# Four one-word loads behind the second pair's stores, and which completion semaphores the later stores get

## The chip, the cores and the metric

One core of one Trainium2 chip. The metric is the device time of one execution in microseconds; the kernel before takes 126.50 us (median of three runs, 126.49 to 126.56). Runs are marked fast or slow (a run over 1.5% above the fastest of the same kernel is slow), and only fast ones are compared. A profiled execution also gives a *span*, some 1.8 us shorter than the time, in which all positions below are counted.

## The reference

```python
def reference(x, weight):            # x: 16 x 64 x 64 x 64, weight: 128 x 64 x 3 x 3, 90% zeros
    x_pad = np.pad(x, ((0, 0), (0, 0), (1, 1), (1, 1)))
    for b, co, ci, kh, kw in ...:
        if weight[co, ci, kh, kw] != 0:
            output[b, co] += weight[co, ci, kh, kw] * x_pad[b, ci, kh:kh+h, kw:kw+w]
```

It is a 3x3 convolution with padding 1. The kernel treats it as dense.

## The kernel before

Two images make a pair; eight pairs follow each other. Input comes by GpSimd's queue, which casts to bf16 on the way (15.73 MB in FP32 by the shapes, 7.86 MB in its packets); output leaves by SyncE's queue, 2 MB for each image.

```python
    const_pool = ctx.enter_context(tc.tile_pool(name="const", bufs=1))
    x_pool = ctx.enter_context(tc.tile_pool(name="x", bufs=1))
    ...
    o_pool = ctx.enter_context(tc.tile_pool(name="o", bufs=7))
    ...
    nc.sync.dma_start(out=w_sb, in_=weight.rearrange("o i kh kw -> o (i kh kw)"))
    x_head = o_pool.tile([128, H, W], FP32, name="o")
    nc.sync.dma_start(out=x_head[:, 0:HEAD, :], in_=pair(0)[:, 0:HEAD, :])
    ...
    for p in range(NP):
        o = [o_pool.tile([C_OUT, H, W], FP32, name="o") for _ in range(2)]
        last = p == NP - 1
        for blk in range(4):
            ...                                   # products on TensorE, sums on VectorE into o
            if last and blk % 2 == 1:
                for n in range(2):
                    rows = slice(r0 - 16, r0 + 16)
                    nc.sync.dma_start(out=out[2 * p + n][:, rows, :], in_=o[n][:, rows, :])
        if not last:
            for n in range(2):
                nc.sync.dma_start(out=out[2 * p + n], in_=o[n])
```

What the source does not show: in the built program every transfer that SyncE issues takes the next of eight completion semaphores, its *slot*, in turn, and waits first for the transfer that had the slot before (the trace's records of its 20 transfers name the semaphores). After its last store SyncE waits for the slots 0, 1, ..., 7 in this order (116.25 to 123.85 us), and only then, at 123.97 us, does it join the closing barrier of all engines.

## Time and profile before

| | before |
|---|---|
| time, median | 126.50 us |
| span | 124.7 us |
| last addition on VectorE ends | 112.0 us |
| last data packet ends | 123.12 us |
| last completion lands | 123.59 us |
| from there to the end of the span | 1.155 us |

How the DMA time is divided, from the queue part of the page (packets, MB, share of 16 engines' span):

```profile
q1 hardware_dynamic: 2880, 34.90, 66.6%
q0 software_dynamic: 1296, 7.86, 30.8%
...
HBM read 17.07 MB, written 33.55 MB: 406 GB/s over the span
```

q1 is SyncE's queue, q0 GpSimd's. Together they fill 97% of the sixteen engines' span, so no idle stretch is left that earlier issues could fill; what can become shorter are the fixed ends.

### The profile page before, as it was taken

What the parts mean: (1) busy time and instruction counts of PE and PEld (TensorE: products, weight loads), DVE (VectorE), ACT (ScalarE), POOL (GpSimd) and SP (SyncE); (2) the same over time, 40 slices, a digit from 0 to 9 for tenths busy, and PEclk for the clock granted to TensorE, in tenths of its full rate; (3) what the DMA queues carried; (4) which work ended last, traced back from release to release, by engine and by line L of the source; (5) the groups of instructions that cost most, each with busy time, mean ns of one, the idle gap of its engine ahead of it and who ended that gap; (6) DMA issues with size and microseconds to landing.
All of it is one profiled execution on the core that took longest, in us unless ns stands there. A gap on an engine that the chain in (4) does not pass through costs nothing.

```text
span 124.7 us, 2543 instructions
## 1 busy us (share of the span) xinstructions
PE 109.0 (87%) x1030; PEld 59.5 (48%) x1030; DVE 82.3 (66%) x135; ACT 39.0 (31%) x71; POOL 41.1 (33%) x46
## 2 busy tenths in 40 slices
PE   6999999999999999999999999999999999940000
PEld 6755555555555555555555555555555555510000
DVE  0354777877787778777877787778777878870000
ACT  4545323333333333333333333333333333300000
POOL 6427343533353335333533333333333300000000
PEclk9999999999999999999999999999999999998555
DMA  4999999999999999999999999999999999999991
GB/s 127 356 225 213 215 218 213 211 400 311 350 409 410 318 297 344 436 310 323 302 433 310 318 315 423 420 449 420 426 431 420 436 426 441 415 412 420 428 381 53
DMA packets 4188, 42.93 MB, mean 344 GB/s; under 512 B 464, under 2 KB 464, under 8 KB 976
## 3 DMA queue, kind: packets, MB, share of 16 engines
q1 hardware_dynamic: 2880, 34.90, 66.6%
q0 software_dynamic: 1296, 7.86, 30.8%
q8 instruction: 8, 0.13, 0.4%
q14 instruction: 4, 0.03, 0.1%
HBM read 17.07 MB, written 33.55 MB: 406 GB/s over the span
## 4 chain that ended last, share of the span: by engine, by line
PE 82%; DMA 5%; DVE 1%; issue 1%; DVEq 0%; SPq 0%
PE ps L148 82%; DMA o<-in_x_dram 5%; DVE o L181 1%; DVEq L233 0%; DVE x L99 0%; SPq L60 0%; DVEq L181 0%
## 5 line engine op out<-in xcount | busy, mean ns | idle before, releaser
L181 DVE TENSOR_TENSOR o<-ps,pc 128x512 f32<-128x512 f32 x124 | 77.8, 686 | 22.1 <-PE ps L148 19.8
L148 PE MATMUL ps<-x,wT 64*128 64x504 bf16 (+3 forms) x780 | 88.7, 373 | 0.3 <-DVE x L99 0.3
L148 PEld LDWEIGHTS <-wT 64*128 64x128 bf16 x966 | 54.4, 94 | 48.9 <-issue 0.3
L167 POOL TENSOR_TENSOR s<-x 128x512 bf16<-128x512 bf16 x31 | 35.6, 1151 | 57.5 <-PE ps L148 43.2
L174 ACT COPY pc<-ps 128x512 f32<-128x512 f32 x62 | 33.3, 589 | 64.0 <-issue 61.8
L148 PE MATMUL ps<-s,wT 64*128 64x512 bf16 (+1 forms) x186 | 25.7, 377 | 0.0
L84 PE MATMUL ps<-idle_rhs 128*128 128x128 bf16 x55 | 4.8, 265 | 1.0 <-DVE idle_rhs L79 1.0
L84 PEld LDWEIGHTS <-idle_rhs 128*128 128x128 bf16 x55 | 4.4, 123 | 1.0 <-DVE idle_rhs L79 1.0
L68 POOL DMA_DIRECT2D x<-in_x_dram x8 | 4.4, 561 | 0.0
L103 DVE CAST w_bf<-w_sb 128x192 bf16<-128x192 f32 (+1 forms) x4 | 1.1, 346 | 2.9 <-DMA w_sb<-in_weight_dram 2.9
L162 DVE COPY o<-ps 128x512 f32<-128x512 f32 x2 | 1.4, 692 | 2.0 <-PE ps L148 2.0
L161 ACT COPY o<-ps 128x512 f32<-128x512 f32 x2 | 1.2, 586 | 2.4 <-PE ps L148 2.4
L99 ACT CAST x<-o 128x576 bf16<-128x576 f32 (+1 forms) x2 | 1.5, 804 | 0.8 <-DMA o<-in_x_dram 0.8
L99 DVE CAST x<-o 128x576 bf16<-128x576 f32 x1 | 0.5, 460 | 1.9 <-DMA o<-in_x_dram 1.9
L103 ACT ACT_TABLE_LOAD x1 | 1.3, 1283 | 0.7 <-PEq L222 0.7
L109 PE MATMUL ps<-ident,w_bf 128*128 128x128 bf16 x9 | 1.1, 296 | 0.3 <-DVE w_bf L103 0.3
L103 ACT CAST w_bf<-w_sb 128x64 bf16<-128x64 f32 (+1 forms) x2 | 0.7, 416 | 1.8 <-DMA w_sb<-in_weight_dram 1.8
L109 PEld LDWEIGHTS <-w_bf 128*128 128x128 bf16 x9 | 0.8, 128 | 0.7 <-DVE w_bf L103 0.7
L113 DVE TENSOR_TENSOR wT<-ps,wT 128x384 bf16<-128x384 f32 x2 | 1.0, 548 | 0.0
L63 POOL DMA_DIRECT2D x<-in_x_dram x1 | 0.7, 693 | 0.8 <-POOLq L222 0.8
L79 DVE MEMSET idle_rhs<- 128x64 uint32 x1 | 0.1, 112 | 0.8 <-PEq L222 0.8
L122 ACT CAST wT<-ps 128x384 bf16<-128x384 f32 x1 | 0.5, 480 | 0.4 <-PE ps L109 0.4
(8 smaller groups left out, 2.0 us busy)
## 6 DMA issues: line engine op xcount, KB each, us to landing
out_dram<-o SPq DMA_DIRECT2D x14, 2048.0 KB, 17.4
x<-in_x_dram POOLq DMA_DIRECT2D x6, 1024.0 KB, 15.8
out_dram<-o SPq DMA_DIRECT2D x4, 1024.0 KB, 11.4
o<-in_x_dram SPq DMA_DIRECT2D x1, 1024.0 KB, 5.6
x<-in_x_dram POOLq DMA_DIRECT2D x1, 640.0 KB, 14.0
x<-in_x_dram POOLq DMA_DIRECT2D x1, 512.0 KB, 7.5
x<-in_x_dram POOLq DMA_DIRECT2D x1, 384.0 KB, 24.6
w_sb<-in_weight_dram SPq DMA_DIRECT2D x1, 288.0 KB, 3.0
```

Source lines behind the costliest of these rows:

```text
L68: nc.gpsimd.dma_start(out=xs[p][:, a:b, :], in_=pair(p)[:, a:b, :])
L84: nc.tensor.matmul(idle_ps, idle_rhs, idle_rhs, start=True, stop=True)
L99: copy(out=xs[0][:, a:b, :], in_=x_head[:, a:b, :])
L103: copy(out=w_bf4[:, g, a:b, :], in_=w_v[:, k : k + b - a, :])
L109: nc.tensor.matmul(wps[:, j, :], src, ident, start=True, stop=True)
L113: nc.vector.tensor_tensor(out=wT[:, g], in0=wps, in1=wT[:, G1], op=SUB)
L148: nc.tensor.matmul(ps[n][:, lo:hi, c_lo:c_hi], tap(g, kw, n), src[q, a:b:step, c_lo + kw - 1 : c_hi + kw - 1], start=(i == 0), stop=(i == ...
L161: nc.scalar.copy(out=o[0][:, r0 : r0 + rows, :], in_=ps[0])
L162: nc.vector.tensor_copy(out=o[1][:, r0 : r0 + rows, :], in_=ps[1])
L167: nc.gpsimd.tensor_tensor(out=s, in0=xs[p][:, r0 : r0 + 16 : 2, :], in1=xs[p][:, r0 + 1 : r0 + 16 : 2, :], op=ADD)
L174: nc.scalar.copy(out=c, in_=shared[n])
L181: nc.vector.tensor_tensor(out=o[n][:, first : r0 + 16 : 2, :], in0=ps[n], in1=pc[n], op=ADD)
```

## The change

The intent: four transfers with as good as no data push all later transfers on SyncE's queue four slots on.

```diff
         if not last:
             for n in range(2):
                 nc.sync.dma_start(out=out[2 * p + n], in_=o[n])
+        if p == 1:
+            spare = const_pool.tile([1, 4], FP32, name="spare")
+            for k in range(4):
+                nc.sync.dma_start(out=spare[:, k : k + 1], in_=weight[0:1, 0, 0, 0:1])
```

The last four stores have slots 0 to 3 before and 4 to 7 after. As a side effect the tile moves all x and o tiles by 32 bytes.

## The prediction

> **What bounds the kernel now.** I read the head of the page first, then the slices, the DMA queues, the chain that ended last, what SyncE's queue waited for, and last a table by stretches of time.
>
> ```profile
> PE 109.0 (87%) x1030; PEld 59.5 (48%) x1030; DVE 82.3 (66%) x135; ACT 39.0 (31%) x71; POOL 41.1 (33%) x46
> ...
> PE   6999999999999999999999999999999999940000
> ...
> DMA  4999999999999999999999999999999999999991
> ```
>
> Two resources look full. TensorE is at 9 from the second slice on, but its last four slices (12.5 us) are empty; the DMA engines are at 9 from the second slice to the last but one. What stands at the end decides.
>
> ```profile
> PE 82%; DMA 5%; DVE 1%; issue 1%; DVEq 0%; SPq 0%
> ...
> 7.35 102.09 PE ps L148 x954
> ...
> 111.38 0.60 DVE o L181
> ```
>
> The chain is 82% TensorE, which invites "TensorE-bound". But it ends at 111.98 us with the last addition, and the span is 124.7 us. The remaining 12.7 us are no engine's work:
>
> ```profile
> 112.00:122.80 10.80, 0.00 (x0) 0.00 (x0) 0.00 (x0) 0.00 (x0) 0.00 (x0) 0.62 0.90 379
> 122.80:123.59 0.79, 0.00 (x0) 0.00 (x0) 0.00 (x0) 0.00 (x0) 0.00 (x0) 0.50 0.03 10
> 123.59:124.70 1.11, 0.00 (x0) 0.00 (x0) 0.00 (x0) 0.00 (x0) 0.00 (x0) 0.50 0.00 0
> ```
>
> Here the engines' columns are all zero; the last two columns are the DMA share and GB/s. DMA is busy to 122.8 us, then there is a completion delay, then 1.1 us in which nothing moves. The volume agrees: 17.07 MB read plus 33.55 MB written is 50.6 MB, in about 120.8 us (2.0 to 122.8), which is 419 GB/s; stretches late in the run (80 to 112 us) show 426. So I take the kernel as bound by the DMA engines nearly from first to last, with TensorE just ahead of them. The fixed end comes after that.
>
> ```profile
> SPq L207 <- DVE o L181: 90.1, 14, 20.1
> SPq L233 <- DMA out_dram<-o: 10.4, 4, 3.2
> SPq L204 <- DVE o L181: 10.1, 4, 4.9
> ```
>
> SyncE, which issues all stores, waits before each store for VectorE's result and for nothing else (14 + 4 waits). No store was ever held by a completion semaphore. Only the program's closing waits are DMA waits: four of them, 10.4 us. The closing waits of SyncE in 123.60 to 123.88 us:
>
> ```profile
> L233 SPq EVENT_SEMAPHORE  x5: 28/28/28, 123.6 to 123.8; - x5
> ```
>
> The trace has their starts at 123.607, 123.666, 123.728, 123.787 and 123.849 us: the first is the wait that the last store ended, the other four found their semaphores long satisfied and cost 59 to 65 ns each.
>
> [...] The trace agrees on the queueing: stores take a median 17.4 us to land though one moves in about 4.9 us (2 MB at 425 GB/s). [...]
>
> **The change part by part.**
>
> *The slots.* The built program hands HWDGE transfers eight completion semaphores in turn, and each transfer first waits for the one that had its slot eight transfers before. Before, weight and first input took slots 0 and 1, the 18 stores 2 to 7, 0 to 7, and 0 to 3. After, four loads take 6, 7, 0, 1 behind the second pair; the last four stores then have slots 4 to 7.
>
> *Waits before stores.* The third pair's two stores now wait for the first pair's (landed at 34.7 and 41.0 us), at 47.4 us, when VectorE releases them. The fourth pair's (60.2 us) wait for the second pair's (50.2 and 56.8 us). The fifth pair's and sixth pair's wait for the four loads, issued about 36 us, so done by some 57 us, against 73.0 and 85.8 us. The seventh pair's (98.6 us) wait for the third pair's (61.4 to 64.8 and 68.5 to 73.3 us). The last four wait for the same stores as before. Every wait is satisfied by 3 us or more: cost 0. VectorE's own waits for free output buffers name other semaphores but the same stores; the order of instructions is the same on all engines but SyncE.
>
> *The four loads themselves.* SyncE's time: it issues stores in 0.33 to 1.35 us and idles from about 36 us to 47 us, so four issues of such a size, 1.3 to 5.4 us, are hidden. Engine time: the smallest records in before's trace are four-byte ones, 9 to 12 ns on the hardware queue (semaphore writes) and 22 ns on the software queue. Four loads of a data and a semaphore record, by those, are 4 x (22 + 12) = 0.14 us[...]. The last store's 16 completions are spread over 2.61 us, and the slowest stands 0.28 us behind the next. So by chance, with one engine in sixteen being the last, the expected cost is about 0.01 us, and at the worst 0.14 us by this estimate.
>
> *The end.* SyncE closes by waiting for slots 0 to 7 in this order (with others that are done). Before, the last four stores sit in slots 0 to 3, so the four satisfied waits for 4 to 7 come after the last landing, on the path: 4 x 61 ns = 0.24 us. After, the satisfied slots 0 to 3 are passed while stores drain, and the wait for slot 7 is the last. Gain 0.24 us of the 1.1 us.
>
> *The spare tile.* Built, it takes 32 bytes of each partition below the x and o tiles; x0 moves from 24704 to 24736 and the first o tile from 101504 to 101536. [...]
>
> Sum: -0.24 + 0.01 + 0.08 = -0.15 us; 126.50 - 0.15 = 126.35, which I put down as 126.3 since I trust the first term most.
>
> **The rivals.**
>
> *Stores issue earlier, because waits are re-paired.* This is what the title suggests at first reading. If slot waits held stores, a gap of several microseconds in DMA could close. Against it: 18 of 18 store waits are VectorE's, and the DMA row has no gap to be filled. It would make nothing of the time.
>
> *Tiny loads are dear.* [...] Against: packets overlap in the trace (the DMA share reads 1.03 in places)[...]. I give this 2%.
>
> *A new wait.* The loads could land so late that the fifth pair's stores wait. They would need to take 37 us (36 to 73); no transfer in the trace took over 25.3. If so, only SyncE waits, behind a DMA queue that still holds the pair before, and little is lost.
>
> *The 32-byte shift changes the rate.* If all transfers lost 1%, that is 1.2 us, 127.5: still within 2%. Nothing in the profile speaks for it[...].
>
> **Range and chances.** The runs of before lie within 0.07 us (126.49 to 126.56). The gain is bounded by 0.24 us unless something unforeseen happens, the costs mostly by 0.3; other chips and builds may move it by 0.3% (0.4 us). So 125.9 to 126.9 for 8 in 10. Two per cent is 2.5 us: only dear loads get there. Faster 0.01, within 0.97, slower 0.02.
>
> **What would show it.** Four store waits at the end ended by DMA as before, and the last of them followed at once by the drain: one closing semaphore wait of SyncE's, not five, behind the last landing, and 0.9 us from it to the end instead of 1.15. SyncE's waits for stores still all on VectorE. DMA still full to about 122.8 us, PE busy 109.0. Wrong would be: a DMA wait at L207; the last store's landing later than 123.6 us by more than 0.3; or the same 1.1 us of silence at the end.

The sum came to -0.24 + 0.01 + 0.08 = -0.15 us, so 126.35. The +0.01 us is an estimate, a sixteenth of 4 x (22 + 12) ns = 0.14 us; the 0.14 us is the worst case, all four loads on the engine that finishes last, which no record shows. The 0.3% for other chips was an allowance: the medians of the kernel before on three chips were 126.50 to 126.61 us.

## The result, and the profile after

126.35 us, median of six runs, against 126.50 us of the kernel before in the same rounds; one of the six is slow, and the median of the five fast ones is 126.21 us. Ratios here are the mean time of one kernel's fast runs over that of the other's in the same rounds, so not quite the ratio of the medians; this one is 0.9985, with a 95% interval of 0.997 to 1.0. The slow run took 131.57 us; such a run also came to the kernel before, in a later comparison (130.8 us), and the ratios leave them out.

The same three stretches at the end, from a table by stretches (columns: us; busy time of TensorE, its weight loads, VectorE, ScalarE, GpSimd with counts; clock; DMA share; GB/s):

```profile
112.00:122.80 10.80, 0.00 (x0) 0.00 (x0) 0.02 (x1) 0.00 (x0) 0.00 (x0) 0.60 0.90 381
122.80:123.41 0.61, 0.00 (x0) 0.00 (x0) 0.00 (x0) 0.00 (x0) 0.00 (x0) 0.50 0.00 0
123.41:124.32 0.91, 0.00 (x0) 0.00 (x0) 0.00 (x0) 0.00 (x0) 0.00 (x0) 0.50 0.00 0
```

The bulk is the same (0.90 of the DMA engines, 381 for 379 GB/s). The silent last stretch is 0.91 us where it was 1.11 in the same view (1.155 and 0.912 us from the records, from the last landing). The closing waits of SyncE between 123.40 and 123.70 us:

```profile
L240 SPq DRAIN  x2: 7/7/7, 123.5 to 123.6; - x2
...
L240 SPq EVENT_SEMAPHORE  x1: 28/28/28, 123.4 to 123.4; - x1
```

One semaphore wait and then at once the drain; before there were five. SyncE comes to its closing waits ten microseconds earlier, while the stores drain (113.0 to 113.3 us):

```profile
L240 SPq EVENT_SEMAPHORE  x4: 28/28/28, 113.1 to 113.2; - x4
```

The first of these four is a wait for other semaphores, the next three (113.12 to 113.25 us) are those for slots 0 to 2. Slot 3 was not yet free: it ended at 113.65 us, with the seventh pair's second store (landed at 113.63 us), and this cost nothing, as four stores were still to land.

What SyncE's queue waited for in the whole run (us in total, times, longest):

```profile
SPq L207 <- DVE o L181: 85.7, 14, 20.2
SPq L240 <- DMA out_dram<-o: 10.0, 5, 2.4
SPq L204 <- DVE o L181: 9.9, 4, 4.8
SPq L207 <- DMA out_dram<-o: 0.8, 1, 0.8
```

The last line is new: once SyncE did wait for a slot ahead of a store. The records tell which: at 49.4 us it had issued the third pair's stores and went on to the wait for the second pair's first store, which landed at 50.125 us; it passed at 50.142. The store behind it was due at 60.2 us, so this wait lies within one for VectorE and cost nothing.

The loads:

```profile
L214 SPq DMA_DIRECT2D spare<-in_weight_dram x4: 1008/1300/1453, 36.1 to 39.8; - x4
```

They took SyncE 5.2 us to issue (36.07 to 41.27 us), in a gap that lasts to 47.4 us, and landed at 52.97 to 53.52 us, 13.7 to 16.9 us after each was issued. Between each load's issue and this landing its semaphore shows exactly two updates, the first 0.12 to 0.17 us after the issue ends and the second 12.1 to 15.6 us later. (A store's shows sixteen.) Who wrote which the trace does not say.

### The profile page after: what moved, and what is told of

The parts are those of the page before. It is cut to its first block, busy times and chain, and to the rows that moved or that the text cites. A ratio compares the mean times of both kernels' runs of the same rounds, so it can differ in the third digit from the quotient of the medians.

```text
span 124.3 us, 2549 instructions
## 1 busy us (share of the span) xinstructions
PE 108.9 (88%) x1030; PEld 59.8 (48%) x1030; DVE 82.2 (66%) x135; ACT 39.0 (31%) x71; POOL 41.1 (33%) x46
## 3 DMA queue, kind: packets, MB, share of 16 engines
q1 hardware_dynamic: 2888, 34.90, 66.8%
## 4 chain that ended last, share of the span: by engine, by line
PE 82%; DMA 5%; DVE 1%; issue 1%; DVEq 0%; SPq 0%
PE ps L148 82%; DMA o<-in_x_dram 5%; DVE o L181 1%; DVEq L240 0%; DVE x L99 0%; SPq L60 0%; DVEq L181 0%
```

## The experiments

Twelve kernels, each in five rounds beside the kernel before on the same chip (its medians were 126.61, 126.58 and 126.50 us, each on another chip; the first covers four_again to five_loads, the second eight_loads to split_stores, the third the other four). "Behind" is the number of closing semaphore waits of SyncE from the one that the last landing ends; "tail" is the time from the last landing to the end of the span, of the profiled run. The medians include slow runs; without them they are 126.21 us for the changed kernel, 126.58 for twelve_loads, 126.61 for pe_later, 127.08 for split_stores and 132.6 for split_rows.

| run | last stores' slots | loads | median us | ratio to before, 95% | behind | tail us |
|---|---|---|---|---|---|---|
| before | 0-3 | 0 | 126.50 | | 5 | 1.155 |
| changed kernel | 4-7 | 4 | 126.35 | 0.9985 (0.997 to 1.0) | 1 | 0.912 |
| four_again | 4-7 | 4 | 126.38 | 0.9983 (0.9969 to 0.9998) | 1 | 0.899 |
| loads_no_shift | 4-7 | 4 | 126.22 | 0.9972 (0.9959 to 0.9985) | 1 | 0.903 |
| tile_only | 0-3 | 0 | 126.39 | 0.9989 (0.9976 to 1.0002) | 5 | 1.145 |
| five_loads | 5-7, 0 | 5 | 126.77 | 1.0016 (1.0003 to 1.003) | 8 | 1.341 |
| eight_loads | 0-3 | 8 | 126.51 | 0.9995 (0.9983 to 1.0007) | 5 | 1.140 |
| twelve_loads | 4-7 | 12 | 126.94 | 1.0017 (0.9988 to 1.0046) | 1 | 0.904 |
| pe_later | 0-3 | 0 | 126.65 | 0.9998 (0.9983 to 1.0012) | 5 | 1.154 |
| split_stores | 4-7 | 0 | 127.10 | 1.0039 (1.0027 to 1.0051) | 1 | 0.898 |
| split_rows | 4-7 | 0 | 136.0 (132.5 to 141.3) | 1.0476 (1.0444 to 1.0509) | 1 | 0.898 |
| twenty_loads | 4-7 | 20 | 126.75 | 1.002 (0.9986 to 1.0054) | 1 | 0.904 |
| twentyeight_loads | 4-7 | 28 | 126.40 | 0.9988 (0.9968 to 1.0007) | 1 | 0.927 |
| four_own_pool | 4-7 | 4 | 126.25 | 0.9974 (0.9956 to 0.9991) | 1 | 0.899 |

My theory was the closing order: the gain is the satisfied waits that no longer stand behind the last landing. The rivals: the loads or the moved tiles gain in themselves; the spread of runs; and, for the premise, that TensorE and not DMA sets the end.

### The change once more

Edit: none.

> The changed kernel itself, once more on this chip. Theory (closing order: the four satisfied waits of 59 to 65 ns leave the path): 0.24 us under the kernel before, ratio about 0.998; one closing semaphore wait after the last landing. Rival (spread of runs only): no difference, ratio 1.000.

Measured: 126.38 us, ratio 0.9983; one wait behind, tail 0.899 us. The gain came back in the size of the first comparison, and this interval lies wholly below 1, narrowly (0.9998).

### Loads without moving the tiles

```diff
+    spare_pool = ctx.enter_context(tc.tile_pool(name="spare", bufs=1))     # after o_pool
...
-            spare = const_pool.tile([1, 4], FP32, name="spare")
+            spare = spare_pool.tile([1, 4], FP32, name="spare")
```

> The same four loads into a tile that lies behind the o tiles, so no other tile moves by 32 bytes. Theory: all of the gain stays, about -0.24 us. Rival (the 32-byte move did it): no gain, 126.5. [...]

Measured: 126.22 us, ratio 0.9972, and later with other rivals once more:

> Four loads behind the second pair with their tile behind the o tiles, once more, on the same chip as its rivals here: 126.2 by the earlier run, one closing wait behind the last landing. Rival (the earlier 126.22 against 126.38 was chance): 126.4.

126.25 us, ratio 0.9974. The gain doesn't need the move of the tiles. By the ratios it is 0.35 and 0.33 us here. That it is more than the 0.24 us of the tail isn't shown, since a ratio of 0.9981 lies in both intervals; nor is it shown to be more than in the changed kernel, as the intervals overlap (0.9956 to 0.9991 for the two here, 0.9969 to 0.9998 for the repeat).

### The tile without loads

```diff
     make_identity(nc, ident)
+    spare = const_pool.tile([1, 4], FP32, name="spare")
+    nc.gpsimd.memset(spare, 0.0)
```

> The spare tile alone, written once by GpSimd at the start, no load; all later tiles 32 bytes further. Theory: closing waits as before (five in a row behind the last landing)[...]. Rival (the 32-byte move did it): 126.3.

Measured: ratio 0.9989 with an interval that includes 1; its closing waits between 123.51 and 123.80 us:

```profile
L235 SPq EVENT_SEMAPHORE  x5: 28/28/28, 123.5 to 123.8; - x5
```

Five behind the landing, tail 1.145 us, as before. No cost of the move was seen; a gain of up to 0.24% isn't excluded by the interval, but the tail didn't take part in it. The expectation on record was about 126.5 us; the range that is cut from it rested on a cost of the move that no trace shows. Nor do the packets show one: of the 1792 packets of 16384 bytes, 1242 took exactly 611 ns before, 1238 in the changed kernel and 1241 here.

### Five loads: the worst order

```diff
-            for k in range(4):
+            for k in range(5):                     # tile of 5 words, in spare_pool
```

> Five loads in place of four, tile behind the o tiles. The last store then has slot 0, the first in the closing order, and seven satisfied waits (1 to 7) stand behind it. Theory: 3 x 61 ns = 0.18 us over the kernel before, 126.7, and 0.43 us over the four loads. Rival (loads or their place gain time in themselves): same as with four, 126.3.

This is the sharpest test, since one load more should turn the gain into a loss. Measured: 126.77 us, ratio 1.0016, which is 0.20 us more by the ratio and 0.16 by the medians (126.61 for the kernel before); 0.18 was expected. The waits of SyncE, and its closing semaphore waits between 123.96 and 124.43 us:

```profile
SPq L241 <- DMA out_dram<-o: 10.7, 1, 10.7
SPq L208 <- DMA out_dram<-o: 10.2, 3, 6.8
```

```profile
L241 SPq EVENT_SEMAPHORE  x8: 28/28/28, 124.0 to 124.4; - x8
```

SyncE stands 10.7 us at the wait for slot 0, which the very last store ends, and then passes eight waits in a row, the other seven long satisfied. From the landing to the drain that is 0.511 us, against 0.324 with five and 0.081 with one: (0.511 - 0.081) / 7 = 0.061 us for each satisfied wait. The rival that loads gain in themselves falls.

The second line shows another rival for the loss: with five loads each store waits for a more recent transfer, and the third pair's second store, which the kernel before issued at 47.98 us, was held by its slot and issued at 50.90 us, 2.9 us later. It doesn't explain the loss: from 44 to 62 us the DMA share stays at 0.98 to 1.05, and the rates of that stretch add up to 6.01 MB against 6.03 before, an estimate of 0.05 us. twentyeight_loads is a harder test: there the fifth pair's stores were issued at 76.05 and 77.12 us in place of 72.99 and 73.59, behind loads, and the time is 0.15 us over that with four loads, all that 24 more loads cost included. With other stores still in the queue, stores issued some 3 us late cost next to nothing here.

### Eight loads: the slots turned full circle

```diff
-        if p == 1:
+        if p in (1, 4):                            # four loads each, in spare_pool
```

> Four loads behind the second pair and four behind the fifth, tiles behind the o tiles: the slots are back where the kernel before has them for the last four stores (0 to 3). Theory: the gain is gone, 126.5 (+0.0 to +0.1 for the loads), five closing waits behind the last landing. Rival (loads in themselves gain): 126.3 or less.

Measured: 126.51 us, ratio 0.9995; between 123.60 and 123.88 us:

```profile
L241 SPq EVENT_SEMAPHORE  x5: 28/28/28, 123.6 to 123.9; - x5
```

The gain is gone with the old slots, though there are twice the loads.

### What a load costs: twelve, twenty and twenty-eight

```diff
-        if p == 1:
+        if p in (0, 1, 4):                         # twelve_loads
```
```diff
+    early = spare_pool.tile([1, 12], FP32, name="early")      # behind x_head's load
+    for k in range(12):
+        nc.sync.dma_start(out=early[:, k : k + 1], in_=weight[0:1, 0, 0, 0:1])
...
+        if p in (1, 4):                            # twenty_loads; (1, 2, 3, 4) for twentyeight_loads
```

> Four loads behind each of the first, second and fifth pair: the last stores have slots 4 to 7 as with four loads, and three times the loads. Theory (a load costs next to nothing): 126.3, within 0.1 us of four loads. [...] at 0.034 us each, as estimated, by 0.4 us on one engine, at most 126.6.

(The 0.4 us is an estimate, 12 x 0.034 us, if all fall on one engine.)

Twelve loads: the tail is that of slots 4 to 7 (0.904 us), but the fast runs fall in two groups: 126.35, 126.48 and 126.58, and 127.31 and 127.36. The profiled run was one of the low ones. In its trace, as in the others with loads, four loads in a row land 0.18 to 0.19 us apart (92.060, 92.247, 92.430, 92.613), five times what I had put down for one. My guess was that a load holds its engine for so long, and that with twelve the engine sometimes becomes the last. The next two kernels were to show it:

> Twelve loads at the very start and four each behind the second and fifth pair; last stores in slots 4 to 7. Theory A (a load takes one engine 184 ns, the spacing at which consecutive loads land): 20 x 0.184 = 3.7 us on that engine; the 16 completions of the last store are 2.5 us apart, so the end moves by 1.2 us (that engine first) to 3.7 us (last): 127.4 to 129.9. Theory B (the spacing is only latency, the engine works on beside it; 0.034 us each as predicted): 126.3 to 126.9.

> Twelve loads at the start and four behind each of the second to fifth pairs; same slots. Theory A: 8 x 0.184 = 1.47 us over the kernel with twenty, 129 to 131. Theory B: 126.3 to 127.2.

Measured: 126.75 us with twenty (six runs from 126.19 to 127.60), 126.40 us with twenty-eight (126.37 to 126.64). Theory A falls: 28 x 0.184 = 5.2 us on one engine would stand out by at least 2.6 us, as the sixteen completions of the last store are only 2.6 us apart in the kernel before. The time with 28 loads is 0.15 us over that with four (126.40 and 126.25), so even if their engine was the first to finish, they set it back by no more than 2.6 + 0.15 us, which is an estimate of at most 0.1 us a load. Both steps take all loads to use the same engine, which is the assumption: no record names the engine. If it holds, the 0.184 us is the rhythm of landings, not the price; it was not shown.

The loads as such don't explain the upper group of twelve_loads or the scatter of twenty_loads, because more of them scatter less. In the profiled run of twenty_loads (127.37 us) the first input landed 1.5 us later (TensorE's products begin at 8.91 us and not at 7.35), and the packets of SyncE's queue in 22 to 36 us moved 24.0 bytes/ns against 26.3 before. But fifteen of the last store's sixteen completions are in by 123.21 us (123.31 in the kernel before), and one alone comes 1.04 us behind them, at 124.25, and makes this run long. Whose it is, and why, is open; split_stores, without loads, has the same picture.

### TensorE 2 us later

```diff
         last = p == NP - 1
+        if p == 5:
+            late_ps = psum_pool.tile([128, 128], FP32, name="ps")
+            for _ in range(32):
+                nc.tensor.matmul(late_ps, idle_rhs, idle_rhs, start=True, stop=True)
```

> The kernel before with 32 idle 128x128 matmuls in front of the sixth pair, some 2 us of TensorE in the middle of the run; no loads. Theory (bound by the DMA engines, which still have over 9 us of stores queued when VectorE ends): the same, 126.5, and only VectorE's end moves, from 112.0 to 114.0 us. Rival (TensorE's chain sets the end): +2 us, 128.5.

Measured: ratio 0.9998. The last step of the chain that ended last:

```profile
113.41 0.60 DVE o L181
```

It was at 111.38 us before. The engines end 2.03 us later and the time stays: TensorE, 82% of "the chain that ended last", isn't what ends last.

### The same slots without loads

```diff
-            if last and blk % 2 == 1:
+            if (last or p < 2) and blk % 2 == 1:
...
-        if not last:
+        if not last and p >= 2:
```

> No loads: the stores of the first two pairs are issued in halves, four transfers more, all of them useful, and the last four stores get slots 4 to 7 as in the changed kernel. Theory: the same gain of 0.24 us, 126.3 (earlier stores share the DMA engines with loads, which move no fewer bytes for it). Rival (the loads matter, not the slots): 126.5.

Measured: 127.10 us, ratio 1.0039: a miss. The tail did as the theory has it (one wait, 0.898 us), but the last landing is at 124.34 us, 0.75 later than before. The DMA engines were busy for 122.69 us each in the mean, against 121.95: the 0.74 us were made by the transfers. In part by shorter rows: a packet of 8192 bytes takes 309 ns and one of 16384 takes 611, so two halves cost 7 ns more than a whole, and 4 stores x 8 rows an engine (128 over 16, in the mean) x 7 ns is an estimate of 0.22 us. The rest isn't explained; of the last store's sixteen completions fifteen are in by 123.36 us (123.31 before), and one alone stands 0.98 us behind (0.28 before). So I cut along partitions next, with whole rows:

```diff
+            cuts = ((0, 64), (64, 128)) if p < 2 else ((0, 128),)
             for n in range(2):
-                nc.sync.dma_start(out=out[2 * p + n], in_=o[n])
+                for a, b in cuts:
+                    nc.sync.dma_start(out=out[2 * p + n][a:b], in_=o[n][a:b])
```

> No loads: each store of the first two pairs is issued as two, partitions 0 to 63 and 64 to 127, so rows stay 16 KiB long; four transfers more, last four stores in slots 4 to 7. Theory (slots matter, and the stores in halves lost by their 8 KiB rows): 126.25, the gain of 0.24 us without a load's cost. Rival (more transfers cost as such): 127.1 as with the stores in halves.

Measured: 132.54 to 141.26 us in six runs, of which two count as fast; the ratio 1.0476 is of these two. The run scatters so widely (clocks 0.907 to 0.947) that only its direction is to be relied on. Again the tail is the short one (0.898 us) and the loss is in the transfers. While the half stores are under way, before and in this kernel, in the table by stretches:

```profile
22.00:35.00 13.00, 13.00 (x126) 6.86 (x122) 10.23 (x17) 4.49 (x10) 5.31 (x6) 1.00 1.02 321
```

```profile
22.00:35.00 13.00, 13.00 (x125) 6.92 (x122) 10.23 (x17) 4.49 (x9) 5.30 (x6) 1.00 1.02 253
```

The engines' work is the same and the DMA share is the same 1.02, but 253 GB/s move in place of 321: each packet takes longer. On SyncE's queue a packet moved 17.6 bytes/ns from 22 to 36 us, where it was 26.3. The mechanism was not looked for further. Here the halves cost 4.8% of the time by the ratio of the two runs that count as fast. What it shows: nearly empty transfers were the cheap way to move the slots, and useful ones weren't.

## Why the prediction was right

**The bound.** Shown by pe_later: 2 us of TensorE in the middle cost no more than 0.15 us by the interval, so TensorE does not set the end; the stores that still drain then do.

**The closing order, -0.24 us.** Shown. The tail is 0.90 to 0.93 us in all nine profiles with one wait behind the landing, 1.14 to 1.155 in the four with five, and 1.34 with eight. The changed kernel's tail became 1.155 - 0.912 = 0.243 us shorter. Times follow: a gain with four loads (four comparisons of four, of which the first has an interval that reaches 1.0), none with eight, a loss with five. One detail was off: slot 3 was still waited for when SyncE came to it, without cost.

**The waits before stores, 0.** Right in the time, wrong in one statement. The prediction held that all of SyncE's waits at stores would stay VectorE's and called a DMA wait there a sign of error. There is one, of 0.8 us. The step behind it compared each landing with the time at which the store was due, and that is the right comparison for the cost; but SyncE comes to a slot's wait earlier, as soon as the store ahead is issued. So the sign was badly chosen, not the step. In five_loads and twentyeight_loads stores really went out late, by 2.9 and up to 3.5 us, and the DMA engines did not run dry: the cost of 0 stands on firmer ground than the reason given for it, that all waits are long satisfied.

**The loads, 0.01 us.** No cost of four was seen, and 28 cost 0.15 us over four. The changed kernel has eight four-byte packets more on SyncE's queue (2888 packets against 2880), two for each load as the prediction had it, and all four-byte packets of that queue took 9 to 25 ns. (The prediction had read 9 to 12 ns for them; in the trace of the kernel before 242 of 320 took 9 ns, 77 took 22 and one 25.) That makes 0.02 to 0.05 us of a load's packets, around the 0.034 us put down; what a load costs its engine besides is at most 0.1 us in all, by the estimate above and its assumption of one engine. To issue a load took SyncE 1.0 to 1.45 us in the changed kernel (36 to 41 us), 0.26 us for single ones in twelve_loads and twentyeight_loads, and 0.22 to 0.33 us for each of the twelve at the start of twenty_loads.

**The moved tiles, +0.08 us.** Wrong: tile_only wasn't slower than before, and the long packets take 611 ns with and without the move. Four loads without the move ran 0.14 and 0.11 us under the changed kernel's repeat, by the ratios, which lies within the intervals.

**The sum.** -0.15 us predicted; 0.9985 and 0.9983 measured, some 0.2 us. That the median is the predicted 126.35 is luck: it includes the slow run, and one term of the sum is wrong. Without that term the sum is -0.23 us, which the intervals allow as well. What stays open is whether the kernels with their own pool gain some 0.1 us beyond the tail. Last landings in profiles point the same way (123.41, 123.44, 123.55 and 123.47 us with four loads; 123.59, 123.51 and 123.60 with none, the tile alone, and eight), but the two groups overlap.

**A version that beats both.** Four loads with their tile behind the others: 126.22 and 126.25 us, 0.3% under the kernel before. Its lead over the changed kernel isn't established.

## What to carry to other kernels

Look at what stands behind the last landing: here eight closing waits in a fixed order, of which those for long finished transfers cost 61 ns each if they come after the one that matters, and nothing if they come ahead. Here it was worth 0.24 us of the tail to have the last transfer in the slot that is waited for last, and one transfer more (five_loads) put it in the first, with a tail 0.19 us longer than before. This was 0.2% of the time; with the DMA engines full from start to end (97% of the span), the re-pairing of waits was not shown to give more than this fixed end.
